# Two pairs of up-projection chunks per FFN in seven products for eight, and another beginning of the first FFN

## The chip, the cores and the metric

The kernel runs on one core of one Trainium2 chip. The metric is device time in microseconds of one execution; the lower, the better. The kernel before takes 1345.03 us (median of three runs, 1344.71 to 1345.4).

## What is computed

Two layers of a decoder trunk, for 256 tokens of width 1024, all in fp32. The change touches the two feed-forward networks (FFNs) of each layer, four in all:

```python
def swiglu(x, w1, w3, w2):
    return (jax.nn.silu(x @ w1) * (x @ w3)) @ w2
...
    for i in range(DEPTH):
...
        h = h + 0.5 * swiglu(rms_norm(h, g_ffn1[i]), w1_a[i], w3_a[i], w2_a[i])
        u = rms_norm(h, g_mix[i])
        h = h + hybrid_mixer(u, w_in[i], g_cq[i], g_ckv[i], w_uq[i], w_ukv[i],
...
        h = h + 0.5 * swiglu(rms_norm(h, g_ffn2[i]), w1_b[i], w3_b[i], w2_b[i])
        ple_gate = jax.nn.sigmoid(rms_norm(h, g_ple[i]) @ w_ple_gate[i])
        h = h + ple_gate * (p[i] @ w_ple_proj[i])
    return rms_norm(h, g_final)
```

DEPTH is 2, w1 and w3 are 1024 x 2816 and w2 is 2816 x 1024. `rms_norm` scales each token by one over its root mean square, and by a gain per channel.

## The kernel before

**Split numbers.** Every fp32 product is made of three matmuls on parts: a number is rounded to a high part, and the low part is the rest. `load` (L74 to 87) brings a weight tile of 128x1024 by a DMA that SyncE issues into `raw` (4 buffers). ScalarE casts it to `whi` (L85), VectorE subtracts to get `wlo` (L86); each has 7 buffers. `mm3` (L94 to 97) issues whi·xhi, wlo·xhi and whi·xlo, each a matmul of 128x512 for one K tile of 128. `split_T` (L126 to 129) does the same for tiles that are no weights.

**An FFN** (`ffn`, from L179). The 2816 columns are 11 chunks of 256. `up(c)` multiplies the tokens (two blocks of 128, `tb`) by the 256 columns of w1 and the 256 of w3 of a chunk: two PSUM banks of 128x512 from a pool of two (`mm`), each of 8 K tiles and 24 matmuls. The token's norm factor `r` is not in x: it is applied afterwards, in silu on ScalarE (L203, `act`) and in the gating on VectorE (L205, `pr`). `turn(c)` transposes the gated tile by four TensorE transposes into a bank of another pool of two (`tr`, L216) and splits it to `fhi` and `flo` (L128, L129). `down` multiplies by two tiles of w2 and adds up into four `acc` banks, which live for the whole FFN: 24 matmuls of 128x512 per chunk. So each chunk has 72 such matmuls and a turn.

**The order.** The loop goes through the chunks: up(c), turn(c-1), down(c-2). After the last chunk come turn(10), and down of chunks 9 and 10 together, bank by bank, chunk 9 ahead in each (L248 to 261); behind each bank the residual is added to h. The framework's scheduler puts the instructions of each engine in a fixed order, in which each engine then works them off, waiting on semaphores; TensorE, ScalarE, VectorE, GpSimd (POOL) and SyncE's DMA queue each have such a list of their own.

**The beginning** (`start`, L783 to 804). The first FFN's x comes transposed from a copy in memory (`xT`, four DMAs of 128x512), each followed by half of the first chunk's weights in pieces of 128x512. ScalarE and VectorE split x, scaled by the gain (L133, L134). The squares (`xsq`) are added up on POOL, and `start_r` (L807 to 816) sums them over the partitions by small matmuls with ones (L813), to get r. `soon` (L818) brings the identity matrix and h after chunk 1, `later` (L824) the constants of the mixer after chunk 3.

**Other places touched.** `ple_in` (L714) loads the embedding of the layer; `_layout` (L842) arranges the inputs on the host.

Of the kernel before, what the change touches and what calls it, by code (L numbers as in the profile page):

```python
# [8 lines left out]
F32 = mybir.dt.float32  # L9
# [5 lines left out]
P = 128  # L15
L = 2
# [17 lines left out]
def trunk(ctx: ExitStack, tc: tile.TileContext, a: dict, out: bass.AP):  # L34
# [26 lines left out]
    gcol = const("gcol", [P, L, 4, KT])  # L61
# [12 lines left out]
    def load(src, n=U, pool=None, step=U):  # L74
# [11 lines left out]
            V.tensor_tensor(out=lo[:, c], in0=raw[:, c], in1=hi[:, c].bitcast(F32), op=ALU.subtract)  # L86
        return hi, lo


    def behind(ins, table):  # L90
# [3 lines left out]
    def mm3(o, lhs, rhs, first, last):  # L94
        PE.matmul(o, lhs[0], rhs[0], start=first, stop=False)  # L95
        PE.matmul(o, lhs[0], rhs[1], start=False, stop=False)  # L96
        PE.matmul(o, lhs[1], rhs[0], start=False, stop=last)  # L97

    def bank(tag, bufs):
        return ps.tile([P, 512], F32, tag=tag, name=nm(tag), bufs=bufs)  # L100
# [1 line left out]
    def bank_mm():  # L102
        return bank("mm", 2)
# [4 lines left out]
    def bank_acc():  # L108
        return bank("acc", 4)
# [66 lines left out]
            pend.pop()()  # L176


    def ffn(li, w13, w2, r, g, first=False, aside=None):  # L179
        with tc.tile_pool(name=nm("fp"), bufs=3) as fp:  # L180
            if first:
                sq, un0 = start(fp)
            acc = []
            ffT = {}

            def up(c):
                nonlocal r
                un = un0 if first and c == 0 else [load(w13[li, c, i]) for i in range(4)]
                fhi = fp.tile([P, 2, S], F32R, tag="fhi", name=nm("fhi"), bufs=4)
                flo = fp.tile([P, 2, S], F32R, tag="flo", name=nm("flo"), bufs=4)  # L190
                ffT[c] = (fhi, flo)
                prs = []
                for tb in range(TB):
                    o = bank_mm()
# [5 lines left out]
                    if r is None:  # L200
                        r = start_r(sq)
                    act = fp.tile([P, FC], F32, tag="act", name=nm("act"))
                    A.activation(act, o[:, :FC], AF.Silu, scale=r[tb])  # L203
                    pr = fp.tile([P, FC], F32, tag="pr", name=nm("pr"), bufs=4)
                    V.scalar_tensor_tensor(  # L205
                        out=pr, in0=o[:, FC:], scalar=r[tb], in1=act, op0=ALU.mult, op1=ALU.mult
                    )
                    prs.append(pr)
                return prs

            def turn(c, prs):
                fhi, flo = ffT[c]
                t = bank_tr()
                for tb in range(TB):
                    for j in range(2):
                        PE.transpose(t[:, j * S + tb * P : j * S + (tb + 1) * P], prs[tb][:, j * P : (j + 1) * P], ident)  # L216
                split_T(t.rearrange("p (j t) -> p j t", j=2), fhi, flo)

            def load2(cs):
                return {c: [load(w2[li, 2 * c + j]) for j in range(2)] for c in cs}  # L220

            def down(cs, un, tb, n):
                for c in cs:
                    for j in range(2):
                        kt = 2 * c + j
                        f = [x[:, j, tb * P : (tb + 1) * P] for x in ffT[c]]
                        w = [x[:, n * 512 : (n + 1) * 512] for x in un[c][j]]
                        mm3(acc[2 * tb + n], f, w, kt == 0, kt == 2 * NFC - 1)

            prs = {}  # L230
            for c in range(NFC):
                prs[c] = up(c)
                if first and c == 1:
                    soon()
                if first and c == 3:
                    later()
                if c == 5 and aside is not None:
                    aside()
                if c == 1:
                    acc.extend(bank_acc() for _ in range(4))  # L240
                if c >= 1:
                    turn(c - 1, prs[c - 1])
                if c >= 2:
                    un = load2([c - 2])
                    for tb in range(TB):
                        for n in range(2):
                            down([c - 2], un, tb, n)
            turn(NFC - 1, prs[NFC - 1])  # L248
            cs = [NFC - 2, NFC - 1]
            un = load2(cs)  # L250
            ro = []
            for tb in range(TB):
                for n in range(2):
                    down(cs, un, tb, n)
# [458 lines left out]

    def ple_in(li, pool):  # L714
        pT = [pool.tile([P, 2, S], F32R, tag=f"pT{i}", name=nm("pT")) for i in range(2)]
        praw = pool.tile([P, 2, S], F32, tag="praw", name=nm("praw"))
        nc.sync.dma_start(praw, a["pT"][li])
        split_T(praw, *pT)
        return pT
# [60 lines left out]
                )  # L780
                nc.sync.dma_start(out[tb * P : (tb + 1) * P, 512:D], o[:, 512:D])

    def start(pool):  # L783
# [4 lines left out]
        un, sq = [], []  # L788
        for k in range(0, KT, 2):
            t = pool.tile([P, 2, S], F32, tag="xraw", name=nm("xraw"), bufs=4)  # L790
            nc.sync.dma_start(t, a["xT"][:, k : k + 2, :])
            q = pool.tile([P, 2, S], F32, tag="xsq", name=nm("xsq"), bufs=4)
            for j in range(2):
                split_g(
                    t[:, j, :].rearrange("p (b t) -> p b t", b=TB), xhi[:, :, k + j, :], xlo[:, :, k + j, :],
                    gcol[:, 0, 0, k + j : k + j + 1],
                )
            un.append(load(a["w13a"][0, 0, k // 2], step=512))
            if k < KT - 2:
                A.activation(q, t, AF.Square)  # L800
            else:
                V.tensor_tensor(out=q, in0=t, in1=t, op=ALU.mult)
            sq.append(q)
        return sq, un


    def start_r(sq):  # L807
        for t in sq[1:]:
            G.tensor_tensor(out=sq[0], in0=sq[0], in1=t, op=ALU.add)
        o = bank_acc()  # L810
        for tb in range(TB):
            for j in range(2):
                PE.matmul(o[:, tb : tb + 1], sq[0][:, j, tb * P : (tb + 1) * P], ones[:, 0:1], start=j == 0, stop=j == 1)  # L813
        ss = small("ss0", 2)
        V.tensor_copy(ss, o[:, 0:2])
        return [rsqrt_mean(ss[:, tb : tb + 1], D) for tb in range(TB)]

    def soon():  # L818
        nonlocal ident
        ident = const("ident", [P, P])  # L820
        for tb in range(TB):
            tc.keep_in_program_order(nc.sync.dma_start(h[tb], a["x"][tb * P : (tb + 1) * P, :]))
# [19 lines left out]
def _layout(i):  # L842
# [4 lines left out]
    c = np.ascontiguousarray  # L847
    o = {}
    o["x"] = c(f["x"].reshape(S, D))
    o["xT"] = c(f["x"].reshape(S, KT, P).transpose(2, 1, 0))  # L850
    o["pT"] = c(f["p"].reshape(L, S, 2, P).transpose(0, 3, 2, 1))

    def tiles(w, kk, ncol):
# [5 lines left out]
    for s in "ab":  # L859
        w1 = f[f"w1_{s}"].reshape(L, D, NFC, FC)  # L860
        w3 = f[f"w3_{s}"].reshape(L, D, NFC, FC)
        o[f"w13{s}"] = tiles(np.concatenate([w1, w3], 3).reshape(L, D, 2 * FF), 2, 512)
        o[f"w2{s}"] = c(f[f"w2_{s}"].reshape(L, 2 * NFC, P, D))
    win = f["w_in"]
    o["wz"] = c(win[:, :, :672].reshape(L, KT, P, 672))
    dq, dk, dv = (win[:, :, 672 + 512 * j : 672 + 512 * (j + 1)] for j in range(3))
# [55 lines left out]
```

## Time and profile before

| | |
|---|---|
| median of three runs | 1345.03 us |
| the profiled execution: its time | 1345.25 us |
| the profiled execution: its span | 1343.2 us |
| mean granted TensorE clock | 0.999 |
| moved by DMA | 236.61 MB, mean 176 GB/s |
| first three turns of the first FFN, in the chain of waits | at 33.13, 44.50 and 61.31 us |

The span goes from the first to the last instruction; 2.05 us of the time lie around it. In the rows of the trace, the first number is the start (in a timeline) and the second the length; `out<-in` names the tiles, `x` the count, and what stands in brackets is how long the engine had been idle, and what ended that. A matmul's recorded length is longer than its share of the pipelined engine: the distance between starts is what it costs.

```profile
PE   8999999999999999999999999999999999999997
DVE  6655565666768655555765555666766676555555
ACT  5544456665775644444654444566667836444445
DMA  7855547534455565555455555474444465655542
```

Each digit is the busy share of a fortieth of the span, in tenths.

### The profile page before, as it was taken

Reading aid. Unit: us, or ns where it says so; the run is one execution under the profiler, and the core shown is the slowest. Engines: PE = TensorE matmul, PEld = TensorE weight load, DVE = VectorE, ACT = ScalarE, POOL = GpSimd, SP = SyncE. Lnnn points to the kernel's source line nnn. Section 1 sums busy time; section 2 is a strip of 40 time slices with the busy share of each in tenths; the row PEclk is TensorE's granted clock in tenths of the full one; section 3 lists DMA queues with packets and bytes.
Section 4 is the critical chain, followed back from the end, with each engine's and each line's share of the span. In section 5 each row is a group of like instructions: output and inputs, shape, how many; then the busy total and the mean of one; then the engine's idle time right before and its main releaser. Section 6 shows DMA issues by size and latency. Waiting matters only on the chain.

```text
span 1343.2 us, 17893 instructions
## 1 busy us (share of the span) xinstructions
PE 1331.4 (99%) x6720; PEld 1114.3 (83%) x6720; DVE 816.0 (61%) x1190; ACT 735.2 (55%) x1122; POOL 50.3 (4%) x110
## 2 busy tenths in 40 slices
PE   8999999999999999999999999999999999999997
PEld 6888889978888888888888888898888788888886
DVE  6655565666768655555765555666766676555555
ACT  5544456665775644444654444566667836444445
POOL 2000000001100000000100000000010000000000
PEclk9999999999999999999999999999999999999999
DMA  7855547534455565555455555474444465655542
GB/s 269 275 187 188 187 131 222 176 112 144 138 170 173 167 207 188 188 187 189 159 188 188 188 188 188 133 224 138 157 141 143 142 208 160 199 189 191 184 158 82
DMA packets 68342, 236.61 MB, mean 176 GB/s; under 512 B 8224, under 2 KB 8864, under 8 KB 68256
## 3 DMA queue, kind: packets, MB, share of 16 engines
q1 hardware_dynamic: 67824, 234.43, 53.7%
q8 instruction: 52, 0.85, 0.3%
q10 hardware_dynamic: 432, 1.05, 0.2%
q14 instruction: 34, 0.28, 0.1%
HBM read 234.40 MB, written 1.05 MB: 175 GB/s over the span
## 4 chain that ended last, share of the span: by engine, by line
PE 95%; DVE 1%; ACT 1%; DMA 1%; issue 0%; SPq 0%; POOL 0%; POOLq 0%; ACTq 0%
PE mm L95 21%; PE mm L97 21%; PE mm L96 21%; PE acc L95 8%; PE acc L97 8%; PE acc L96 8%; PE tr L216 1%; PE tr L143 1%; PE tr L512 1%; DVE wlo L86 1%; ACT whi L85 1%; PE acc L614 1%; PE acc L596 1%; PE acc L486 1%; DMA xraw<-in_xT 1%; PE tr L475 0%
## 5 line engine op out<-in xcount | busy, mean ns | idle before, releaser
L86 DVE TENSOR_TENSOR wlo<-raw,whi 128x1024 fp32r<-128x1024 f32 (+3 forms) x450 | 534.0, 1200 | 252.8 <-ACT whi L85 235.5
L85 ACT CAST whi<-raw 128x1024 fp32r<-128x1024 f32 (+3 forms) x450 | 456.5, 1029 | 260.2 <-PE acc L97 134.9
L95 PE MATMUL mm<-whi,xhi 128*128 128x512 f32 (+1 forms) x1032 | 403.7, 392 | 1.7 <-ACT whi L85 1.2
L96 PE MATMUL mm<-wlo,xhi 128*128 128x512 f32 (+1 forms) x1032 | 401.7, 390 | 0.7 <-DVE wlo L86 0.7
L97 PE MATMUL mm<-whi,xlo 128*128 128x512 f32 (+1 forms) x1032 | 401.7, 389 | 0.0
L95 PEld LDWEIGHTS mm<-whi,xhi 128*128 128x128 f32 x1032 | 193.8, 188 | 43.1 <-ACT whi L85 1.9
L96 PEld LDWEIGHTS mm<-wlo,xhi 128*128 128x128 f32 x1032 | 194.0, 188 | 41.1 <-DVE wlo L86 2.5
L97 PEld LDWEIGHTS mm<-whi,xlo 128*128 128x128 f32 x1032 | 193.8, 188 | 40.2 <-DVE xlo L129 0.9
L95 PE MATMUL acc<-whi,fhi 128*128 128x512 f32 x352 | 140.9, 402 | 0.0
L203 ACT ACTIVATE act<-mm,r 128x256 f32<-128x256 f32 x88 | 41.8, 475 | 176.7 <-PE mm L97 172.5
L97 PE MATMUL acc<-whi,flo 128*128 128x512 f32 x352 | 137.2, 392 | 0.0
L96 PE MATMUL acc<-wlo,fhi 128*128 128x512 f32 x352 | 136.8, 390 | 0.0
L205 DVE SCALAR_TENSOR_TENSOR pr<-mm,r,act 128x256 f32<-128x256 f32 x88 | 42.3, 481 | 130.7 <-ACT act L203 130.7
L97 PEld LDWEIGHTS acc<-whi,flo 128*128 128x128 f32 x352 | 66.0, 188 | 14.7
L95 PEld LDWEIGHTS acc<-whi,fhi 128*128 128x128 f32 x352 | 66.2, 188 | 13.2 <-ACT fhi L128 1.0
L96 PEld LDWEIGHTS acc<-wlo,fhi 128*128 128x128 f32 x352 | 66.3, 188 | 12.7
L95 PE MATMUL mm<-xhi,whi 128*128 128x256 f32 x256 | 73.9, 289 | 0.0
L97 PE MATMUL mm<-xhi,wlo 128*128 128x256 f32 x256 | 72.4, 283 | 0.0
L96 PE MATMUL mm<-xlo,whi 128*128 128x256 f32 x256 | 72.4, 283 | 0.0
L95 PEld LDWEIGHTS mm<-xhi,whi 128*128 128x128 f32 x256 | 48.9, 191 | 2.0 <-ACT eT L514 0.7
L96 PEld LDWEIGHTS mm<-xlo,whi 128*128 128x128 f32 x256 | 49.0, 191 | 0.0
L97 PEld LDWEIGHTS mm<-xhi,wlo 128*128 128x128 f32 x256 | 48.9, 191 | 0.0
(211 smaller groups left out, 1350.9 us busy)
## 6 DMA issues: line engine op xcount, KB each, us to landing
raw<-in_w13b SPq DMA_DIRECT2D x88, 512.0 KB, 4.5
raw<-in_w13a SPq DMA_DIRECT2D x84, 512.0 KB, 4.5
raw<-in_wg SPq DMA_DIRECT2D x48, 512.0 KB, 4.1
raw<-in_w2a SPq DMA_DIRECT2D x44, 512.0 KB, 4.3
raw<-in_w2b SPq DMA_DIRECT2D x44, 512.0 KB, 4.3
raw<-in_wqk SPq DMA_DIRECT2D x32, 512.0 KB, 4.3
raw<-in_wo SPq DMA_DIRECT2D x24, 512.0 KB, 4.3
raw<-in_wv SPq DMA_DIRECT2D x16, 512.0 KB, 4.4
```

The lines of the kernel that those rows point to most:

```text
L85: A.copy(hi[:, c], raw[:, c])
L86: V.tensor_tensor(out=lo[:, c], in0=raw[:, c], in1=hi[:, c].bitcast(F32), op=ALU.subtract)
L95: PE.matmul(o, lhs[0], rhs[0], start=first, stop=False)
L96: PE.matmul(o, lhs[0], rhs[1], start=False, stop=False)
L97: PE.matmul(o, lhs[1], rhs[0], start=False, stop=last)
L143: PE.transpose(t[:, j * P : (j + 1) * P], h[tb][:, k * P : (k + 1) * P], ident)
L203: A.activation(act, o[:, :FC], AF.Silu, scale=r[tb])
L205: V.scalar_tensor_tensor(out=pr, in0=o[:, FC:], scalar=r[tb], in1=act, op0=ALU.mult, op1=ALU.mult)
L216: PE.transpose(t[:, j * S + tb * P : j * S + (tb + 1) * P], prs[tb][:, j * P : (j + 1) * P], ident)
L486: PE.matmul(o[:, P : 3 * P], q[:, P : 2 * P], k, start=True, stop=True)
L512: PE.transpose(t[:, j * P : (j + 1) * P], e[:, j * P : (j + 1) * P], ident)
L596: PE.matmul(os[i][:, c], k, q, start=True, stop=True)
```

## The change

**Pairs of chunks.** Chunks 7 and 8, and chunks 9 and 10, go through one matrix product of 2x2 blocks: the blocks of x are (token block) x (half of the 1024 channels), those of the weights (half of the channels) x (chunk). Seven products of such blocks are made in place of eight, each with 4 K tiles, so 12 matmuls of 128x512 (`products`). That needs sums and differences of blocks. For x they are made once per FFN (`x_forms`), after token block 1 is scaled by the ratio of the two blocks' norm factors, which a matmul of ones with a diagonal matrix spreads over the partitions; so one r serves both token blocks. For the weights, four differences of two tiles each are made per pair on VectorE (`form`), and each of the seven operands is split (`make`). The results are put together by additions of 128x512 that read the PSUM bank (`add`), and one copy on ScalarE.

**Order.** Chunks 0 to 2 go as before. Then come two blocks of eight steps (`block`): in each, seven products alternate with single weight tiles (`up_unit`) of two plain chunks (3 and 4; 5 and 6), and with down units of one w2 tile. At the end stand down(5), turns 6 and 10, down(6), turn 9, and down of chunks 9 and 10, bank by bank.

**Beginning.** x and the weights of chunk 0 come together in eight DMAs of 128x768 (`xw`). r comes from h by `norm_r` as in the other stages; h's two DMAs stand between weight tiles of chunk 1. Chunk 0 keeps its two banks until r is there, and chunk 1 goes into two `acc` banks. The gain comes by ScalarE's DMA queue. `start_r`, the squares and `soon` are gone. The embedding's tile is taken from a pool of scratch tiles.

Core of the diff:

```diff
+            def up_unit(c, i, os):
+                un = load(w13[li, c, i])
+                if i == 0:
+                    os.extend(bank_mm() for _ in range(TB))
+                for tb in range(TB):
+                    for kt in (2 * i, 2 * i + 1):
+                        w = [x[:, (kt % 2) * 512 : (kt % 2) * 512 + 512] for x in un]
+                        mm3(os[tb], x_at(tb, kt), w, kt == 0, kt == KT - 1)
+                if i == 3:
+                    for tb in range(TB):
+                        gated(c, tb, os[tb], r[tb])
...
+            def down_unit(c, j):
+                w = load(w2[li, 2 * c + j])
+                for tb in range(TB):
+                    for n in range(2):
+                        down(c, j, w, tb, n)
...
+            def x_forms():
+                rho = small("rho")
+                V.reciprocal(rho, r[0])
+                V.tensor_tensor(out=rho, in0=rho, in1=r[1], op=ALU.mult)
+                dg = scratch()[:, :P]
+                V.tensor_scalar_mul(dg, ident, rho)
+                o = bank_tr()
+                PE.matmul(o[:, :P], ones, dg, start=True, stop=True)
+                rb = fp.tile([P, P], F32, tag="rb", name=nm("rb"), bufs=1)
+                A.copy(rb, o[:, :P])
...
+                for t, tb, n in ((a10, 1, 0), (a11, 1, 1), (a00, 0, 0), (a01, 0, 1)):
+                    c = slice(4 * n, 4 * n + 4)
+                    V.tensor_tensor(
+                        out=v4(t), in0=xhi[:, tb, c, :].bitcast(F32), in1=xlo[:, tb, c, :].bitcast(F32), op=ALU.add
+                    )
+                    if tb:
+                        V.tensor_tensor(out=v4(t), in0=v4(t), in1=rb[:, None, :].to_broadcast([P, 4, P]), op=ALU.mult)
...
+                V.tensor_tensor(out=s1, in0=a10, in1=a11, op=ALU.add)
+                f[5] = quarter(s1)
+                sub(s1, s1, a00)
+                f[6] = quarter(s1)
+                sub(a10, a00, a10)
+                f[7] = quarter(a10)
+                sub(a01, a01, s1)
+                f[3] = quarter(a01)
+                f[4] = quarter(a11)
...
+                def form(i):
+                    for u, w in enumerate(ws):
+                        if i == 1:
+                            sub(w[0, 0], w[0, 1], w[0, 0])
+                        elif i == 2:
+                            t2s.append(wtile())
+                            sub(t2s[u], w[1, 1], w[0, 0])
+                        elif i == 3:
+                            sub(w[0, 1], w[1, 1], w[0, 1])
+                        else:
+                            sub(w[1, 0], w[1, 0], t2s[u])
...
+                def products():
+                    o = bank_tr()
+                    product(o, 1, True)
+                    m1 = t512("m1")
+                    A.copy(m1, o)
+                    yield
+                    product(o, 2)
+                    gated(c, 0, o, r[0])
+                    yield
+                    o = bank_tr()
+                    product(o, 6, True)
+                    u2 = t512("u2")
+                    add(u2, o, m1)
+                    yield
+                    product(o, 7)
+                    add(m1, o, m1)
+                    yield
...
+                for k in range(8):
+                    if k < 6:
+                        make((2, 6, 7, 5, 3, 4)[k])
+                    if k < 3:
+                        form(k + 2)
...
+                    if k < 7:
+                        next(ps)
...
+                    up_unit(plain[k // 4], k % 4, os)
+                    if k in downs:
+                        down_unit(*downs[k])
+                    for t in turns.get(k, ()):
+                        turn(t)
...
+            for j in range(2):
+                down_unit(5, j)
+            turn(6)
+            turn(10)
+            for j in range(2):
+                down_unit(6, j)
+            turn(9)
+            un = {(c, j): load(w2[li, 2 * c + j]) for c in (9, 10) for j in range(2)}
```

**ScalarE at the end of the first FFN.** Before: `tr_298` is the turn of chunk 9, `tr_305` that of chunk 10, the `whi` are casts of weights.

```order
L203 ACTIVATE act_296_1457<-mm_295_1432,r_31_207 128x256
L85 CAST whi_340_1638<-raw_339_1637 128x1024
L128 CAST fhi_263_1274<-tr_298_1461 128x512
L85 CAST whi_343_1644<-raw_342_1643 128x1024
L85 CAST whi_346_1650<-raw_345_1649 128x1024
L128 CAST fhi_290_1401<-tr_305_1504 128x512
```

Now: `tr_346` is the turn of chunk 6, `tr_349` of chunk 10, `tr_358` of chunk 9.

```order
L86 CAST whi_393_1734<-raw_392_1733 128x1024
L135 CAST fhi_344_1544<-tr_346_1546 128x512
L135 CAST fhi_347_1553<-tr_349_1555 128x512
L86 CAST whi_396_1740<-raw_395_1739 128x1024
L86 CAST whi_399_1746<-raw_398_1745 128x1024
L135 CAST fhi_356_1598<-tr_358_1600 128x512
```

A weight cast stands right ahead of the last turned tile's cast in both. What moved is on TensorE, at the same place. Before, behind the last turn (`tr_305`, its tile is `fhi_290`):

```order
L216 MATMUL tr_305_1504<-ident_326,pr_297_1459 128x128 x2
L95 MATMUL acc_57_330<-whi_307_1512,fhi_263_1274 128x512
L96 MATMUL acc_57_330<-wlo_308_1513,fhi_263_1274 128x512
L97 MATMUL acc_57_330<-whi_307_1512,flo_264_1275 128x512
L95 MATMUL acc_57_330<-whi_310_1518,fhi_263_1274 128x512
L96 MATMUL acc_57_330<-wlo_311_1519,fhi_263_1274 128x512
L97 MATMUL acc_57_330<-whi_310_1518,flo_264_1275 128x512
L95 MATMUL acc_58_331<-whi_307_1512,fhi_263_1274 128x512
L95 MATMUL acc_57_330<-whi_313_1524,fhi_290_1401 128x512
```

Now, around the last turn (`tr_358`, its tile is `fhi_356`):

```order
L102 MATMUL acc_58_321<-whi_354_1581,fhi_344_1544 128x512
L103 MATMUL acc_58_321<-wlo_355_1582,fhi_344_1544 128x512
L104 MATMUL acc_58_321<-whi_354_1581,flo_345_1545 128x512
L250 MATMUL tr_358_1600<-ident_228,pr_252_1111 128x128 x2
L250 MATMUL tr_358_1600<-ident_228,pr_324_1444 128x128 x2
L102 MATMUL acc_55_318<-whi_360_1608,fhi_356_1598 128x512
```

Before, seven matmuls that read an older tile stand between the last turn and the first use of its tile; now none does.

**VectorE at the start of the first block,** second FFN: `pr_1104` is the gated tile of chunk 2, the `wr` are weight tiles of the pair and their forms, the `wlo` splits.

```order
L136 TENSOR_TENSOR wlo_1109_4782<-wr_1076_4665,whi_1108_4781 128x1024
L136 TENSOR_TENSOR wlo_1111_4786<-wr_1080_4669,whi_1110_4785 128x1024
L87 TENSOR_TENSOR wlo_1114_4793<-raw_1112_4791,whi_1113_4792 128x1024
L238 SCALAR_TENSOR_TENSOR pr_1104_4770<-mm_1102_4743,r_1012_4427,act_1103_4768 128x256
L136 TENSOR_TENSOR flo_1106_4773<-tr_1107_4774,fhi_1105_4772 128x512
L320 TENSOR_TENSOR wr_1076_4665<-wr_1077_4666,wr_1076_4665 128x1024
L320 TENSOR_TENSOR wr_1080_4669<-wr_1081_4670,wr_1080_4669 128x1024
L87 TENSOR_TENSOR wlo_1117_4811<-raw_1115_4809,whi_1116_4810 128x1024
L136 TENSOR_TENSOR wlo_1119_4828<-wr_1078_4667,whi_1118_4827 128x1024
L136 TENSOR_TENSOR wlo_1121_4832<-wr_1082_4671,whi_1120_4831 128x1024
```

Where before weight splits and gated tiles alternated, four splits of the pair and two forms now stand among them.

**VectorE in the beginning,** now: `xlo` and the first `wlo` belong to chunk 0, `wlo_23` to `wlo_32` to chunk 1, `pr_46` and `pr_48` are the gated tiles of chunk 0.

```order
L136 TENSOR_TENSOR wlo_16_139<-wr_18_146,whi_15_138 128x512
L293 TENSOR_TENSOR wr_63_331<-xhi_68,xlo_69 128x512
L87 TENSOR_TENSOR wlo_23_204<-raw_21_202,whi_22_203 128x1024
L293 TENSOR_TENSOR wr_64_332<-xhi_68,xlo_69 128x512
L87 TENSOR_TENSOR wlo_26_211<-raw_24_209,whi_25_210 128x1024
L238 SCALAR_TENSOR_TENSOR pr_46_254<-mm_19_152,r_38_239,act_45_252 128x256
L269 RECIPROCAL rho_59_322<-r_38_239 128x1
L270 TENSOR_TENSOR rho_59_322<-rho_59_322,r_44_250 128x1
L87 TENSOR_TENSOR wlo_29_218<-raw_27_216,whi_28_217 128x1024
L238 SCALAR_TENSOR_TENSOR pr_48_258<-mm_20_177,r_44_250,act_47_256 128x256
```

Two weights of chunk 1 (`wlo_29` and the one behind `pr_48`) now stand behind operations that read r; before, r was read behind one of chunk 1's.

More of the change, by code (lines that the diff above doesn't have):

```diff
@@ L87, in load, with split_w @@
         return hi, lo
+    def split_w(w):
+        hi = wp.tile([P, U], F32R, tag="whi", name=nm("whi"), bufs=7)
+        lo = wp.tile([P, U], F32R, tag="wlo", name=nm("wlo"), bufs=7)
+        split_T(w, hi, lo)
+        return hi, lo
     def behind(ins, table):
@@ L92, in behind, with mm3 @@
         tc.add_manual_dep(ins.ins, table.ins.name, order, reason="behind")
[L94 to L97, printed above, removed]
+    def mm3(o, lhs, rhs, first, last, **more):
+        PE.matmul(o, lhs[0], rhs[0], start=first, stop=False, **more)
+        PE.matmul(o, lhs[0], rhs[1], start=False, stop=False, **more)
+        PE.matmul(o, lhs[1], rhs[0], start=False, stop=last, **more)
     def bank(tag, bufs):
@@ L179, in ffn, with wtile, t512, up @@
     def ffn(li, w13, w2, r, g, first=False, aside=None):
+        nonlocal ident
         with tc.tile_pool(name=nm("fp"), bufs=3) as fp:
+            def wtile():
+                return fp.tile([P, U], F32, tag="wr", name=nm("wr"), bufs=10)
+            def t512(name):
+                return fp.tile([P, 512], F32, tag="t512", name=nm(name), bufs=4)
             if first:
-                sq, un0 = start(fp)
+                un0 = start(wtile)
             acc = []
             ffT = {}
[L186 to L192, printed above, removed]
+            prs = {}
+            def up(c, un, bank):
+                os = []
                 for tb in range(TB):
-                    o = bank_mm()
+                    o = bank()
                     for kt in range(KT):
@@ L199, in up, with gated, turn @@
                             settle()
[L200 to L212, printed above, removed]
+                    os.append(o)
+                    if r is not None:
+                        gated(c, tb, o, r[tb])
+                return os
+            def up_unit(c, i, os):
[9 more added lines that the diff above has]
+                        gated(c, tb, os[tb], r[tb])
+            def gated(c, tb, o, scale):
+                act = fp.tile([P, FC], F32, tag="act", name=nm("act"), bufs=2)
+                A.activation(act, o[:, :FC], AF.Silu, scale=scale)
+                pr = fp.tile([P, FC], F32, tag="pr", name=nm("pr"), bufs=6)
+                V.scalar_tensor_tensor(
+                    out=pr, in0=o[:, FC:], scalar=scale, in1=act, op0=ALU.mult, op1=ALU.mult
+                )
+                prs[c, tb] = pr
+            def turn(c):
+                fhi = fp.tile([P, 2, S], F32R, tag="fhi", name=nm("fhi"), bufs=4)
+                flo = fp.tile([P, 2, S], F32R, tag="flo", name=nm("flo"), bufs=4)
+                ffT[c] = (fhi, flo)
                 t = bank_tr()
@@ L222, in down @@
[L222 to L232, printed above, removed]
-                if first and c == 1:
[L234 to L238, printed above, removed]
+            def down(c, j, w, tb, n):
+                kt = 2 * c + j
+                f = [x[:, j, tb * P : (tb + 1) * P] for x in ffT[c]]
+                mm3(acc[2 * tb + n], f, [x[:, n * 512 : (n + 1) * 512] for x in w], kt == 0, kt == 2 * NFC - 1)
@@ new lines, in ffn @@
+            for c in range(3):
+                if first and c == 1:
+                    un = []
+                    for i in range(4):
+                        un.append(load(w13[li, c, i]))
+                        if i < 2:
+                            load_h(i)
+                    ident = const("ident", [P, P])
+                    r = [norm_r(tb) for tb in range(TB)]
+                    for tb, o in enumerate(os0):
+                        gated(0, tb, o, r[tb])
+                    up(c, un, bank_acc)
+                else:
+                    os0 = up(c, un0 if first and c == 0 else [load(w13[li, c, i]) for i in range(4)], bank_mm)
@@ L239, in ffn @@
                 if c == 1:
                     acc.extend(bank_acc() for _ in range(4))
+                    fx = x_forms()
+                    wg = winograd(7, fx)
                 if c >= 1:
[L242 to L249, printed above, removed]
@@ L250, in ffn @@
-            un = load2(cs)
+                    turn(c - 1)
+            wg[0](1)
+            wg[1](1)
+            for j in range(2):
+                down_unit(0, j)
+            if first:
+                later()
+            wg = block(
+                wg, (3, 4), {0: [2], 4: [3]},
+                {0: (1, 0), 1: (1, 1), 2: (2, 0), 3: (2, 1), 5: (3, 0), 6: (3, 1)}, 9,
+            )
+            if aside is not None:
+                aside()
+            block(
+                wg, (5, 6), {0: [4], 1: [7], 2: [8], 5: [5]},
+                {1: (4, 0), 2: (4, 1), 3: (7, 0), 4: (7, 1), 5: (8, 0), 6: (8, 1)},
+            )
@@ L793, in start @@
             for j in range(2):
[L794 to L804, printed above, removed]
@@ L807, in start_r @@
[L807 to L822, printed above, removed]
+                t = wtile()[:, : S + 512]
@@ new lines, in start @@
+                nc.sync.dma_start(t, a["xw"][:, k + j, :])
+                src = t[:, :S].rearrange("p (b t) -> p b t", b=TB)
+                xh, xl = xhi[:, :, k + j, :], xlo[:, :, k + j, :]
+                g = gcol[:, 0, 0, k + j : k + j + 1]
+                if k == 0:
+                    V.tensor_scalar_mul(xh, src, g)
+                    V.scalar_tensor_tensor(
+                        out=xl, in0=src, scalar=g, in1=xh.bitcast(F32), op0=ALU.mult, op1=ALU.subtract,
+                    )
+                else:
+                    split_g(src, xh, xl, g)
```

95 lines of the change are left out of this document (82 added, 13 removed).

## The prediction

> **What bounds the kernel now.** I read the page first: busy time, then the shares of the chain that ended last.
>
> ```profile
> span 1343.2 us, 17893 instructions
> PE 1331.4 (99%) x6720; PEld 1114.3 (83%) x6720; DVE 816.0 (61%) x1190; ACT 735.2 (55%) x1122; POOL 50.3 (4%) x110
> PE 95%; DVE 1%; ACT 1%; DMA 1%; issue 0%; SPq 0%; POOL 0%; POOLq 0%; ACTq 0%
> L86 DVE TENSOR_TENSOR wlo<-raw,whi 128x1024 fp32r<-128x1024 f32 (+3 forms) x450 | 534.0, 1200 | 252.8 <-ACT whi L85 235.5
> ```
>
> TensorE is busy for 99% of the span and is 95% of the chain. VectorE has 39% free and waits mostly for ScalarE's casts. So removed matmuls count in full, as long as VectorE and ScalarE, which get more work, still deliver weights in time. Next, the price of a matmul, from the timeline of TensorE inside one up chunk, and a window over a whole FFN:
>
> ```profile
> 67.07 0.39 PE L95 MATMUL mm<-whi,xhi 128*128 128x512 f32 x1
> ...
> 77.72 0.39 PE L97 MATMUL mm<-whi,xlo 128*128 128x512 f32 x1
> 77.95 0.60 PE L216 MATMUL tr<-ident,pr 128*128 128x128 f32 x4
> 78.31 0.48 PE L95 MATMUL acc<-whi,fhi 128*128 128x512 f32 x1
> ```
> ```profile
> 470.00:640.00 170.00, 170.00 (x771) 140.41 (x771) 88.70 (x94) 75.94 (x94) 0.64 (x3) 1.00 0.58 190
> ```
>
> From 67.07 to 77.72 lie 47 starts, so one 128x512 matmul costs 10.65 / 47 = 0.2266 us, whatever its recorded 0.39. A turn of four transposes costs 78.31 - 77.95 = 0.36. In the window (columns: busy time and count of PE, PEld, DVE, ACT, POOL, then clock, DMA share, GB/s) TensorE never stops, at granted clock 1.00. VectorE is busy 88.7 of 170, and the DMA engines 0.58: there is room for both.
>
> All sums below are made against the profiled execution, 1345.25 us (span 1343.2 and 2.05 around it); the median of the runs is 1345.03, so the two are interchangeable here.
>
> **1. Matmuls removed: -21.75.** A pair of chunks has 2 x 48 = 96 products of the form 128x512; by seven products for eight it has 84. Two pairs in each of four FFNs: 8 x 12 = 96 matmuls fewer, 96 x 0.2266 = 21.75 us.
>
> **2. Work added on TensorE: +0.9.** Each FFN gets one matmul with ones that spreads the ratio of the two norms over the partitions. The nearest row is a chain step of the same shape:
>
> ```profile
> 209.16 0.45 PE tr L279 x4
> ```
>
> Two such matmuls stand in that step; I take 0.22 each, 0.9 for four; bounds 0.4 to 1.8.
>
> **3. Beginning of the first FFN: -4.6.** What it takes now:
>
> ```profile
> 21.70 0.50 PE mm L95
> 33.13 0.44 PE tr L216 x4
> ```
> ```profile
> 16.63 1.05 PE L813 MATMUL acc<-ones,xsq 128*128 128x1 f32 x8 [0.18 <-POOL xsq L809]
> 21.70 0.50 PE L95 MATMUL mm<-whi,xhi 128*128 128x512 f32 x1 [0.48 <-DVE pr L205]
> ```
> ```profile
> 5.40 0.88 DVE L134 SCALAR_TENSOR_TENSOR xlo<-xraw,gcol,xhi 128x256 fp32r<-128x256 f32 x2 [5.40 <-ACT xhi L133]
> 6.37 0.69 DVE L86 TENSOR_TENSOR wlo<-raw,whi 128x512 fp32r<-128x512 f32 x1
> ...
> 13.65 1.78 DVE L86 TENSOR_TENSOR wlo<-raw,whi 128x512 fp32r<-128x512 f32 x1
> 15.35 1.91 DVE L134 SCALAR_TENSOR_TENSOR xlo<-xraw,gcol,xhi 128x256 fp32r<-128x256 f32 x2
> ```
>
> The first turn comes at 33.13, after 96 matmuls worth 21.75. Before, TensorE pays for the norm (16.63: small matmuls; 21.70: no free bank until a gated tile is made), and VectorE's last operations before that took 1.78 and 1.91 for shapes that take 0.69 and 0.88 elsewhere, while POOL added squares. After, POOL's additions of squares and the small matmuls are gone, and chunk 1 goes into other banks. What is late next is VectorE: it begins at 5.4 with 2 scalings and 8 differences of 128x256 (0.44 each, half of the 0.88), 8 subtractions of 128x512 (0.6) and, in the same queue, two of the four additions of the forms (0.6): 4.4 + 4.8 + 1.2 = 10.4, so the last piece is ready at 15.8. The last group of six matmuls then ends at about 17.2, and 48 x 0.2266 = 10.9 us later chunk 1 ends, at 28.1. I add 0.4: behind the gated tile of chunk 0, which waits for the norm, stand two weight subtractions of chunk 1 (see the order), and the norm now waits for h, which arrives between weight tiles. So 28.5 for 33.13: -4.6. Bounds: -5.5 (28.1, and the x-forms' additions hidden) and 0 (the norm 4 us later, at about 25).
>
> **4. End of each FFN: +9.2 in all.** Before, the last turn is covered:
>
> ```profile
> 183.81 0.39 PE L97 MATMUL acc<-whi,flo 128*128 128x512 f32 x1
> ...
> 184.72 0.60 PE L216 MATMUL tr<-ident,pr 128*128 128x128 f32 x4
> 185.07 0.48 PE L95 MATMUL acc<-whi,fhi 128*128 128x512 f32 x1
> ...
> 186.54 0.72 PE L95 MATMUL acc<-whi,fhi 128*128 128x512 f32 x2
> ```
> ```profile
> 184.23 2.00 ACT L85 CAST whi<-raw 128x1024 fp32r<-128x1024 f32 x2 [3.34 <-PE acc L97]
> 186.13 0.58 ACT L128 CAST fhi<-tr 128x512 fp32r<-128x512 f32 x1
> ```
>
> ScalarE starts two weight casts at 184.23, when a matmul frees their buffers, and only then the cast of the turned tile (186.13); TensorE meanwhile does matmuls of the chunk before, until 186.54. After the change, the down units of chunk 6 stand right behind turns 6 and 10, those of chunk 9 right behind turn 9, and need just these turned tiles; nothing else can run. In ScalarE's queue one weight cast, which waits for the last matmul of the preceding down unit, stands ahead of each (the order shows both). For turn 9: the matmul frees the buffer 0.19 after the turn begins (0.39 recorded, less the pitch of 0.2266, and 0.03 from 183.81 + 0.39 to 184.23); cast 0.95 (half of 1.90, from 184.23 to 186.13); turned tile 0.58; so TensorE resumes at 1.74, not 0.36: **1.35 lost** (rounded down, since matmuls read the tile's first half first). For turns 6 and 10 the same 1.74 against 2 x 0.36 = 0.72: 1.0. Sum 2.35 x 4 = 9.4, less some 0.2 of such waiting in before. Bounds: 0 if ScalarE takes its instructions in another order, (2.35 + 2 x 0.95) x 4 = 17 if two casts came ahead each time, as at 184.23.
>
> **5. VectorE at the beginning of the pairs: +4.0.** Per pair of chunks VectorE gets 14 splits instead of 8, and 8 forms, all of 128x1024; per FFN it also gets 25 operations of 128x512 or near it, for the x-forms and for adding up the products. Prices:
>
> ```profile
> 453.23 1.23 DVE L86 TENSOR_TENSOR wlo<-raw,whi 128x1024 fp32r<-128x1024 f32 x1 [1.79 <-ACT whi L85]
> 454.38 1.28 DVE L147 TENSOR_TENSOR xg<-tr,gcol 128x512 f32<-128x512 f32 x2
> 455.57 1.21 DVE L86 TENSOR_TENSOR wlo<-raw,whi 128x1024 fp32r<-128x1024 f32 x1
> 456.71 1.28 DVE L129 TENSOR_TENSOR xlo<-xg,xhi 128x512 fp32r<-128x512 f32 x2
> ```
> ```profile
> L86 DVE TENSOR_TENSOR wlo<-raw,whi 128x1024 fp32r<-128x1024 f32 x420 | 507.4, 1223 | 236.4 <-ACT whi L85 221.4
> L85 ACT CAST whi<-raw 128x1024 fp32r<-128x1024 f32 x420 | 435.1, 1051 | 253.7 <-PE acc L97 133.4 <-PE mm L97 86.8 <-PE mm L96 23.3
> L203 ACT ACTIVATE act<-mm,r 128x256 f32<-128x256 f32 x88 | 41.8, 475 | 176.7 <-PE mm L97 172.5 <-POOL r L124 4.1
> L205 DVE SCALAR_TENSOR_TENSOR pr<-mm,r,act 128x256 f32<-128x256 f32 x88 | 42.3, 481 | 130.7 <-ACT act L203 130.7
> ```
>
> Back to back, a wide operation takes 1.14 (455.57 to 456.71), and one of 512 takes half of 1.20 (454.38 to 455.57 for two); I use 0.62, and 0.45 for 256. Over the whole FFN this fits. Eleven chunks last 11 x (72 x 0.2266 + 0.36) = 183 us, of which VectorE is busy 52% (88.7 of 170), some 95 us; (112 x 1.14 + 99 x 0.62) / 4 = 47 us come on top. The tight place is the start of block 1. From behind the gated tile that ends chunk 1 to the weights of chunk 3's third unit, VectorE's order has 23 wide operations, 14 of 512 and 3 of 256: 23 x 1.14 + 14 x 0.62 + 3 x 0.45 = 36.3 us. TensorE's order has 156 matmuls, three turns and the ones step there: 156 x 0.2266 + 3 x 0.36 + 0.22 = 36.7 us; but VectorE starts 1.1 later, by the matmul's end (0.17 beyond its pitch), 0.475 on ScalarE and the gated tile's own 0.48. So it is 36.3 + 1.1 - 36.7 = 0.7 late in FFNs 2, 3 and 4. In the first a 24th wide operation, a weight of chunk 2, stands in the stretch: 1.9. That makes 3 x 0.7 + 1.9 = 4.0. Bounds: 0, since some of the waiting matmuls can be others', and 26 (the slower side below). Behind this place VectorE has less per unit and gets ahead again. ScalarE has 45% free, and 48 more casts of 1.05 are 12.6 us per FFN; the bytes of the weights do not change.
>
> **Sum:** 1345.25 - 21.75 + 0.9 - 4.6 + 9.2 + 4.0 = **1333.0 us**.
>
> **Rivals.**
>
> *Covers hold (B).* Terms 4 and 5 are nothing: 1345.25 - 21.75 + 0.9 - 4.6 = 1319.8. For it: VectorE at 61%, and the existing FFN end loses next to nothing. Against it: the order leaves TensorE no matmul behind turn 9.
>
> *Full durations (C).* If each wide operation held VectorE for its recorded 1.22 rather than 1.14, the tight place is 23 x 0.08 = 1.85 later in each FFN, 7.4 in all: 1340.4. The rows speak against it, with starts 1.14 apart. For it speaks that the x-forms and forms here often read what the operation just ahead has written, which no quoted pair does. The Trainium skill has this rule in "VectorE: DVE Perf Modes", section "The DRAIN you can't avoid": the next operation does not start until the pipe has emptied, and only one that is not held starts earlier. By the rule the whole kernel would come out at C; the quoted rows, 1.14 apart behind an operation of 1.21, agree with its exception only.
>
> *The start gains nothing (E).* The norm late, as bounded in 3: 1333.0 + 4.6 = 1337.6.
>
> *The slower side (D): each subtraction waits for its own cast.* In before, runs of VectorE's splits are often paced by ScalarE:
>
> ```profile
> 470.62 1.22 DVE L86 TENSOR_TENSOR wlo<-raw,whi 128x1024 fp32r<-128x1024 f32 x1 [0.16 <-ACT whi L85]
> 488.37 3.95 DVE L86 TENSOR_TENSOR wlo<-raw,whi 128x1024 fp32r<-128x1024 f32 x3 [1.45 <-ACT whi L85]
> ```
>
> A form, its cast and its subtraction are one chain across two engines. With 1.22 + 0.16 = 1.38 per wide operation instead of 1.14, the tight place is 23 x 0.24 = 5.5 longer per FFN, 22 in all: 1355.0. It decides from 1.27 on (1345.25 - 1333.0 = 12.25, and 12.25 / 4 / 23 = 0.133 above 1.14); the triple at 488.37 has 3.95 / 3 = 1.32. Against it: forms and x-forms between the splits need no cast and give ScalarE time to get ahead.
>
> *That products aren't saved* can't be: the order counts 4584 matmuls of 128x512 for 4680.
>
> **Chances.** Forecast 0.62 (1327 to 1339 by its own terms), B 0.14, E 0.07, C 0.09, D 0.08. A measurement of this kernel can tell about 0.2%, 2.7 us, from no change, so faster means below 1342.3. Everything but D and the upper edge of C does that: faster 0.88, same 0.05, slower 0.07. The range runs from B to just above C, 1319 to 1341, and leaves out D and half of B.
>
> **What would show it.** Term 1: 96 fewer 128x512 matmuls at an unchanged pitch. Term 3: the first turn near 28.5. Term 4: in each FFN, just ahead of the last two groups of down units, TensorE idle for 1.0 and 1.35 with a cast of the turned tile as releaser. Term 5: waits for a subtraction in the first 37 us after chunk 1, under 1 us per FFN (1.9 in the first), and VectorE at about 1020 us busy. The prediction is wrong if TensorE shows gaps in the middle of the blocks, if the products wait for a bank (the copy or addition that empties it), or if the ends show none.

## The result and the profile after

| | before | after |
|---|---|---|
| median | 1345.06 us (4 runs, 1344.71 to 1345.4) | 1333.43 us (4 runs, 1332.72 to 1334.1) |
| profiled execution | 1345.25 us | 1332.86 us |
| its span | 1343.2 us | 1331.1 us |

The ratio is 0.9913, with a 95% interval of 0.9898 to 0.9928: 0.9% faster. The forecast was 1333.0 us.

The page of the changed kernel, first the span and the busy times, then the shares of the chain that ended last:

```profile
span 1331.1 us, 17969 instructions
PE 1312.2 (99%) x6624; PEld 1097.5 (82%) x6624; DVE 994.0 (75%) x1414; ACT 802.8 (60%) x1205; POOL 50.2 (4%) x109
PE 94%; ACT 2%; DVE 2%; DMA 1%; issue 1%; POOL 0%; SPq 0%; POOLq 0%; ACTq 0%; DVEq 0%
```

TensorE is still the bound: it has 96 instructions less and is 19.2 us less busy. VectorE has 178 us more to do (about 204 were counted) and hides nearly all of it. The view of TensorE's waits lists what is not hidden (total us, times, longest):

```profile
PE acc L102 <- ACT fhi L135: 7.7, 8, 1.2
PE tr L992 <- POOL mhalf L72: 1.0, 1, 1.0
PE acc L103 <- DVE wlo L87: 0.9, 2, 0.5
PE tr L102 <- ACT m L352: 0.6, 1, 0.6
```

Eight waits for a turned tile, two in each FFN, stand out. In before, the same list comes to 4.0 us in all, and no matmul in it waits for `fhi`. The chain of the changed kernel, at the beginning of the first FFN and at its end (start, length):

```profile
18.98 0.57 POOL r L175
...
21.93 0.56 POOL r L175
22.60 1.24 DVE wlo L87
23.88 0.50 PE acc L103
29.41 0.44 PE tr L250 x4
```
```profile
171.78 0.90 ACT whi L86
172.74 0.59 ACT fhi L135
173.37 0.50 PE acc L102
...
179.16 1.04 ACT whi L86
180.20 0.49 ACT fhi L135
180.74 0.50 PE acc L102
```

The first turn begins at 29.41 for 33.13. At the end, each time a weight cast, then the turned tile's cast, and then TensorE: the order that the section on the change shows.

### The profile page after: what moved, and what is told of

Same layout as the page of the kernel before. It is cut to its first block, busy times and chain, and to the rows that moved or that the text cites. A ratio compares the mean times of both kernels' runs of the same rounds, so it can differ in the third digit from the quotient of the medians.

```text
span 1331.1 us, 17969 instructions
## 1 busy us (share of the span) xinstructions
PE 1312.2 (99%) x6624; PEld 1097.5 (82%) x6624; DVE 994.0 (75%) x1414; ACT 802.8 (60%) x1205; POOL 50.2 (4%) x109
## 4 chain that ended last, share of the span: by engine, by line
PE 94%; ACT 2%; DVE 2%; DMA 1%; issue 1%; POOL 0%; SPq 0%; POOLq 0%; ACTq 0%; DVEq 0%
PE mm L102 17%; PE mm L104 17%; PE mm L103 17%; PE acc L102 8%; PE acc L103 8%; PE acc L104 8%; PE tr L104 4%; PE tr L102 4%; PE tr L103 4%; PE tr L250 1%; PE tr L150 1%; ACT whi L86 1%; PE tr L716 1%; DVE wlo L87 1%; DMA h<-in_x 1%
## 5 line engine op out<-in xcount | busy, mean ns | idle before, releaser
L87 DVE TENSOR_TENSOR wlo<-raw,whi 128x1024 fp32r<-128x1024 f32 (+1 forms) x378 | 450.1, 1201 | 137.3 <-ACT whi L86 135.1
L86 ACT CAST whi<-raw 128x1024 fp32r<-128x1024 f32 (+1 forms) x378 | 387.3, 1035 | 198.2 <-PE mm L104 77.5
L102 PE MATMUL mm<-whi,xhi 128*128 128x512 f32 (+1 forms) x760 | 296.0, 393 | 0.0
L103 PE MATMUL mm<-wlo,xhi 128*128 128x512 f32 (+1 forms) x760 | 295.1, 389 | 0.3 <-DVE wlo L87 0.3
L104 PE MATMUL mm<-whi,xlo 128*128 128x512 f32 (+1 forms) x760 | 295.2, 389 | 0.0
L103 PEld LDWEIGHTS mm<-wlo,xhi 128*128 128x128 f32 x760 | 142.9, 188 | 28.9 <-DVE wlo L87 0.8
L135 ACT CAST whi<-wr 128x1024 fp32r<-128x1024 f32 (+1 forms) x120 | 121.6, 1023 | 66.9 <-PE acc L104 38.9
L136 DVE TENSOR_TENSOR wlo<-wr,whi 128x1024 fp32r<-128x1024 f32 (+1 forms) x120 | 140.6, 1185 | 24.8 <-ACT whi L135 23.6
L320 DVE TENSOR_TENSOR wr<-wr,wr 128x1024 f32<-128x1024 f32 x64 | 76.3, 1217 | 0.0
L102 PE MATMUL tr<-whi,q 128*128 128x512 f32 x160 | 63.7, 398 | 0.0
L104 PE MATMUL tr<-whi,q 128*128 128x512 f32 x160 | 62.6, 391 | 0.0
```

The costliest lines, as they stand in the source:

```text
L86: A.copy(hi[:, c], raw[:, c])
L102: PE.matmul(o, lhs[0], rhs[0], start=first, stop=False, **more)
L103: PE.matmul(o, lhs[0], rhs[1], start=False, stop=False, **more)
L104: PE.matmul(o, lhs[1], rhs[0], start=False, stop=last, **more)
L135: A.copy(hi, t)
L136: V.tensor_tensor(out=lo, in0=t, in1=hi.bitcast(F32), op=ALU.subtract)
```

## Experiments

**The saved matmuls put back.** The first product of each pair is issued twice.

```diff
                     product(o, 1, True)
+                    product(o, 1, True)
```

> The first of the seven products is issued twice in each pair (its second start overwrites the first): 8 x 12 = 96 more matmuls of 128x512, the number that the change saves. If TensorE is the bound inside the blocks, each costs 0.2266 us: +21.75 on 1333.4, less what they cover of the waits at the start of block 1 (some 3 us in the trace): 1352 to 1355. Rival: the blocks are bound by VectorE, and a matmul more is hidden there: under +10, below 1343.

Measured: 1352.59 us (1352.34 to 1353.11), +19.2 on the changed kernel. By the marks of the chain (the first transposes behind each FFN) the second, third and fourth FFN are 5.44, 5.45 and 5.41 us longer: 24 x 0.2266 = 5.44, the full price, so the blocks are bound by TensorE. The first FFN is only 3.4 longer. There the added matmuls cover 1.6 of the waits at the start of block 1 (TensorE loses 1.25 from 28 to 75 us, 2.88 in the changed kernel), and the first turn begins 0.4 earlier (29.02 for 29.41).

**The turns at the end moved ahead.**

```diff
-            for j in range(2):
-                down_unit(5, j)
-            turn(6)
-            turn(10)
+            down_unit(5, 0)
+            turn(6)
+            turn(9)
+            down_unit(5, 1)
             for j in range(2):
                 down_unit(6, j)
-            turn(9)
```

Turn 10 goes into the block's list of turns, behind its last unit.

> The last three turns are moved ahead: turn 10 behind the last unit of the block, turns 6 and 9 between the two down units of chunk 5, so that at least 12 matmuls (2.7 us) stand between each turn and the first use of its tile. If the two waits per FFN (1.06 + 1.42 and 0.1 behind each, 2.7) come from ScalarE's weight cast ahead of the turned tile's, they go: -9.5 to -10.8, 1322.6 to 1323.9. Rival: ScalarE's two casts of turned tiles, now ahead, make the weight casts behind them late, and the wait comes back on a weight: less than 3 gained, above 1330.

Measured: 1323.12 us (1322.34 to 1323.19), ratio to the kernel before 0.9837 (0.9823 to 0.9852): 10.3 less than the changed kernel. By the marks behind the FFNs each gives 2.6 to 2.8; 0.8 is lost again in the second layer's mixer, at the same `kf`. The timeline of ScalarE in this run, at the end of the first FFN:

```profile
169.66 1.05 ACT L86 CAST whi<-raw 128x1024 fp32r<-128x1024 f32 x1 [1.31 <-PE acc L104]
170.61 1.07 ACT L135 CAST fhi<-tr 128x512 fp32r<-128x512 f32 x2
173.26 1.05 ACT L86 CAST whi<-raw 128x1024 fp32r<-128x1024 f32 x1 [1.59 <-PE acc L104]
```

A weight cast still stands ahead of the two turned tiles, but they are done at 171.7, and TensorE, which has the second down unit of chunk 5 to do, does not wait at all. The rival falls: no wait came back on the weights. This version beats both kernels.

**VectorE loaded early in the block.**

```diff
                             sub(t2s[u], w[1, 1], w[0, 0])
+                            if c == 7:
+                                sub(t2s[u], w[1, 1], w[0, 0])
```

> The two subtractions of the second form (128x1024) are done twice in the first block: two more wide operations on VectorE per FFN, in the stretch that I called tight. If VectorE has no slack there, each costs its 1.14: 2 x 1.14 x 4 = 9.1, less a few tenths of slack per FFN: +7 to +9, 1340.5 to 1342.5. Rival: the waits there come from one order of semaphores and not from the amount of work: under +1.5.

Measured: 1336.27 us (1335.73 to 1336.75), +2.8: neither 7 nor nothing. By the marks of the chain the four FFNs are 0.4, 0.5, 0.6 and 0.5 longer, and the rest, 1.0, is lost in the second layer's mixer, whose code is the same (a wait of 0.8 for `kf` that the changed kernel does not have). So 2.27 us of work cost 0.5, and some 1.7 us of room were found, of which the expectation had none. In the second FFN TensorE's order shows where: behind the turn in this stretch, twelve matmuls of product 2 stand ahead of the first one that needs a new low part, and four in the changed kernel. Eight more are 1.8 us.

**The same load late in the block.**

```diff
                     fw[i] = [split_w(t2s[u] if i == 6 else w[at[i]]) for u, w in enumerate(ws)]
+                    if c == 7 and i == 4:
+                        for u, w in enumerate(ws):
+                            hi, lo = fw[i][u]
+                            V.tensor_tensor(out=lo, in0=w[1, 0], in1=hi.bitcast(F32), op=ALU.subtract)
```

> The same two wide operations on VectorE per FFN, but at the sixth step of the first block (the low parts of the last operand of the pair are subtracted twice). By my account VectorE is ahead there by 5 us or more: 0, 1333.0 to 1334.0. Rival: VectorE's sum of work is the bound over the whole block: +9, as in the run with the early place.

Measured: 1333.12 us (1332.81 to 1333.32): 0. VectorE's work is free there.

**Twice as much early.** The loop does the second form three times instead of twice.

```diff
-                            sub(t2s[u], w[1, 1], w[0, 0])
+                            for _ in range(3 if c == 7 else 1):
+                                sub(t2s[u], w[1, 1], w[0, 0])
```

> As the run with two more wide operations early in the first block, but four of them per FFN. Two cost 2.84 in all, far less than 9.1; so some 1.6 us of slack per FFN must have been there, and the next two find none: 2 x 1.14 = 2.27 per FFN, +6.8 (three FFNs) to +9.1 (four) on 1336.27: 1343 to 1345.4. Rival: each costs a part, because the scheduler orders other matmuls ahead as it did for two: another +2.8, about 1339.

Measured: 1347.05 us (1345.47 to 1348.09), +10.8 on the run with two, above the range. TensorE's waits in this run, and its timeline in the first FFN:

```profile
PE mm L103 <- DVE wlo L87: 9.5, 4, 2.7
```
```profile
58.36 0.79 PE L103 MATMUL mm<-wlo,xhi 128*128 128x512 f32 x1 [2.67 <-DVE wlo L87]
58.95 0.63 PE L104 MATMUL mm<-whi,xlo 128*128 128x512 f32 x1
59.38 0.63 PE L102 MATMUL mm<-whi,xhi 128*128 128x512 f32 x1
59.80 0.63 PE L103 MATMUL mm<-wlo,xhi 128*128 128x512 f32 x1
```

One wait per FFN, 9.5 us in all. By the marks the second and the fourth FFN are 2.3 longer than with two operations, just the 2 x 1.14 expected; the first and the third are 3.3 and 3.6 longer. What comes on top there is the clock. Behind the wait, matmuls start 0.43 apart and not 0.2266, in the first and the third FFN, though not in the second and fourth. The windows show it (columns as before; the clock is the last but two):

```profile
56.00:58.00 2.00, 0.00 (x0) 0.00 (x0) 2.00 (x3) 1.79 (x2) 0.00 (x0) 1.00 0.00 0
58.00:59.00 1.00, 0.64 (x2) 0.55 (x3) 1.00 (x2) 1.00 (x2) 0.00 (x0) 0.51 0.00 0
59.00:60.00 1.00, 1.00 (x4) 0.81 (x3) 1.00 (x3) 1.00 (x2) 0.00 (x0) 0.50 0.70 94
...
62.00:63.00 1.00, 1.00 (x6) 0.82 (x5) 1.00 (x2) 0.00 (x0) 0.00 (x0) 1.00 0.74 299
```

**The beginning alone.** The kernel before, with the new beginning of the first FFN:

```diff
-                prs[c] = up(c)
-                if first and c == 1:
-                    soon()
+                if first and c == 1:
...
+                    r = [norm_r(tb) for tb in range(TB)]
+                    prs[0] = [gated(o, r[tb]) for tb, o in enumerate(prs[0])]
+                    prs[c] = up(c, un, bank_acc)
```

> The kernel before with only the new beginning of the first FFN (x and weights in one stream, r from h, chunk 0 held in its banks, chunk 1 in two acc banks). The first turn of the changed kernel begins at 29.4, of which 0.2 is the ones step, for 33.1 before: -3.7 to -4.0, since nothing behind it is changed: 1341.0 to 1341.3. Rival: what is gained there is lost again in the next chunks, whose weights come no sooner: -1 or less, above 1344.

Measured: 1340.12 us (1339.83 to 1340.93) beside 1344.91 for the kernel before, ratio 0.9965 (0.9952 to 0.9978): -4.8, more than expected. The first turn comes in two halves in this run, two transposes at 22.54 and two at 27.78; the matmul behind it starts at 27.92 (33.33 in the same view of before, 5.4 later), and the marks behind all four FFNs stay 5.2 to 5.4 ahead. So the beginning by itself gives some 5, and about 1.3 is lost again in the changed kernel, between 21.77 and 24.21, as waits and slow starts that this run does not have. The norm is late there. POOL's first operation of it (128x1) takes 3.05 us in the changed kernel and 0.30 in this run, so that the norm of block 0 is there at 19.54 for 17.20. First the changed kernel, then this run:

```profile
15.48 3.05 POOL L171 TENSOR_SCALAR ss<-ss 128x1 f32<-128x1 f32 x1 [14.53 <-ACT junk L164]
17.26 1.22 DVE L87 TENSOR_TENSOR wlo<-raw,whi 128x1024 fp32r<-128x1024 f32 x1
```
```profile
14.47 1.23 DVE L87 TENSOR_TENSOR wlo<-raw,whi 128x1024 fp32r<-128x1024 f32 x1 [0.58 <-ACT whi L86]
15.45 0.30 POOL L165 TENSOR_SCALAR ss<-ss 128x1 f32<-128x1 f32 x1 [14.49 <-ACT junk L158]
```

POOL's operation ends 0.05 behind VectorE's in both, at 18.53 behind 18.48 and at 15.75 behind 15.70. In the changed kernel VectorE works without a gap up to 18.48, with the x-forms' additions between the splits; here it stops at 15.70. So the x-forms do take the 1.3, but by way of POOL; that VectorE holds POOL up is read from these times and was not tested by itself. Behind the late norm, VectorE multiplies the norms' ratio only at 22.52, and a weight of chunk 1 stands right behind it:

```profile
22.52 0.16 DVE L270 TENSOR_TENSOR rho<-rho,r 128x1 f32<-128x1 f32 x1 [1.89 <-POOL r L175]
22.60 1.22 DVE L87 TENSOR_TENSOR wlo<-raw,whi 128x1024 fp32r<-128x1024 f32 x1
```

**The forms left out.**

```diff
-                        if i == 1:
-                            sub(w[0, 0], w[0, 1], w[0, 0])
-                        elif i == 2:
-                            t2s.append(wtile())
-                            sub(t2s[u], w[1, 1], w[0, 0])
...
+                        if i == 2:
+                            t2s.append(w[1, 1])
```

> The changed kernel without the 64 subtractions of weight tiles that make the forms (the operands of the products are the plain tiles, so what is computed is not the reference's), all splits, products and the x-forms stay. VectorE is freed of 16 x 1.14 = 18 us per FFN. If its work costs only where TensorE waits for a subtraction at the start of block 1, it gives back 0.3 in each of three FFNs and at most 1.7 in the first, whose wait for the copy stays: -0.5 to -2.6, 1330.8 to 1332.9. Rival: the added work on VectorE slows the blocks elsewhere too: -5 or more, below 1328.5.

Measured: 1336.07 us (1335.25 to 1336.76): slower than with the forms, which neither theory had. So something else must have changed with it. ScalarE's timeline in the first FFN, and TensorE's:

```profile
53.03 0.47 ACT L236 ACTIVATE act<-tr,r 128x256 f32<-128x256 f32 x1 [1.98 <-PE tr L104]
53.40 1.98 ACT L86 CAST whi<-raw 128x1024 fp32r<-128x1024 f32 x2
```
```profile
54.49 0.73 PE L102 MATMUL mm<-whi,xhi 128*128 128x512 f32 x2 [1.50 <-ACT whi L86]
55.75 0.50 PE L103 MATMUL mm<-wlo,xhi 128*128 128x512 f32 x1 [0.53 <-DVE wlo L87]
```

The scheduler, with the forms gone, put the activation behind product 2 ahead of two weight casts. ScalarE waited for product 2 for 1.98 us, TensorE then for the weights, and the granted clock was 0.50 from 56.2 to 59.6 us. To see whether that is all, the activation was held behind the casts of the next operand:

```diff
-                    gated(c, 0, o, r[0])
+                    gated(c, 0, o, r[0], casts[-1] if first and c == 7 else None)
...
+                if after is not None:
+                    behind(silu, after)
```

> As the run without the form subtractions (the result is again not the reference's), but in the first FFN ScalarE's activation behind product 2 is held behind the casts of the next operand, where the changed kernel has it. In the run without forms the scheduler had put it ahead of two casts of plain weights; TensorE then waited 1.5 and 0.5 us for them at 54 us, and its clock stood at half for 3 us. If that one place explains the loss, it goes (2.1 us by the marks at the end of that FFN), and the gain of the missing forms shows: 1331 to 1334. Rival: leaving the forms out costs by itself, by an earlier use of buffers or of the DMA: 1335.5 to 1336.5 again.

Measured: 1332.51 us (1331.66 to 1332.72). The loss in the first FFN was that one place. Without the forms, 18 us of VectorE's work per FFN, the first FFN ends 1.7 earlier than in the changed kernel, and the other three gain nothing more; in the second layer's mixer 1.3 of it is lost again, 0.9 of that as a wait for `kf`. The medians are 0.9 apart, the two profiled executions 0.1 (1332.72 and 1332.86). TensorE's loss in the first FFN's stretch from 29 to 65 us falls from 2.85 to 0.94: the forms are what it waits for there. The `kf` wait comes and goes between kernels with the same mixer; its cause stays open.

## Why the prediction was right, point by point

"Saved" and "lost" are sums of starts in TensorE's timeline against the pitch of 0.2266.

| term | forecast | measured | from |
|---|---|---|---|
| 1 matmuls removed | -21.75 | -21.75 | 5.44 per FFN, put back |
| 2 ones step | +0.9 | +0.9 | 0.22 each |
| 3 beginning | -4.6 | -3.9 | 33.13 to 29.41 less the ones step |
| 4 ends of FFNs | +9.2 | +10.3 | 2.7 per FFN, less 0.1 each in before |
| 5 VectorE at block 1 | +4.0 | +3.5 | 2.6 in the first FFN, 0.3 in each other |
| sum | -12.25 | -10.95 | |
| profiled executions | | -12.39 | |

The terms measured leave 1.4 us over. 0.3 is the time around the span (2.05 before, 1.76 after), some 0.4 lies between the FFNs by the marks of the chain, and the rest in differences of 0.1 per FFN that I did not trace. That the forecast of 1333.0 came within 0.4 of the median is therefore partly luck: terms 3 to 5 together were 1.3 too low, and these 1.4 made up for it.

**Term 1** was right, price and place. The pitch of the matmuls is the old one:

```profile
506.60 0.39 PE L102 MATMUL mm<-whi,xhi 128*128 128x512 f32 x1
...
512.49 0.39 PE L104 MATMUL tr<-whi,q 128*128 128x512 f32 x1
```

26 intervals in 5.89 us are 0.2265 each, products of the pair among them.

**Term 3** was 0.7 too large. The step that was mis-sized is the allowance of 0.4 for the norm, which cost 1.3: 0.76 as waits and the rest as slower starts around them, behind POOL's operation of 3.05 us, which the forecast did not have. Chunk 0 itself ended at 16.8 (17.2 worked out), and VectorE's last piece was ready at 15.0 (15.8 forecast). The run of the beginning alone shows the bound of -5.5 (x-forms hidden) to be about what it gives by itself.

**Term 4** was right in mechanism and place, and a little small. Behind turns 6 and 10 TensorE loses 1.06 and then 0.1, behind turn 9 1.42 and 0.1: 2.7 per FFN for 2.35. The chain gives the parts: casts begin 171.78 and 172.74, 0.96 apart, and TensorE starts 0.63 behind the second, for 0.95 and 0.58. The three parts of the forecast (0.19, 0.95 and 0.58) add up to 1.72, not 1.74. The rounding down was wrong, and the first matmul behind a wait costs 0.1 more. That the wait is made by TensorE's order, and not by ScalarE's amount of work, is shown by the run with the turns ahead.

**Term 5** was near in its sum by luck, with errors that cancel. VectorE's time was as counted: in the second FFN it works without a gap from 476.57, behind the gated tile, to 512.91, when the weight in question is ready. That is 36.34 us; 36.3 was forecast.

```profile
476.57 1.29 DVE L297 TENSOR_TENSOR wr<-wr,rb 128x512 f32<-128x512 f32 x2
...
511.69 1.22 DVE L87 TENSOR_TENSOR wlo<-raw,whi 128x1024 fp32r<-128x1024 f32 x1
```
```profile
477.00:515.00 38.00, 38.00 (x172) 31.13 (x172) 37.90 (x43) 24.22 (x30) 0.00 (x0) 1.00 0.66 232
```

VectorE is busy for 37.90 of 38.00 us there, and still TensorE does not stop. The step that failed is "So it is 36.3 + 1.1 - 36.7 = 0.7 late in FFNs 2, 3 and 4": it lets the unit need its low part with its first matmul. In TensorE's timeline three matmuls that need only the high part, or another tile, come first:

```profile
512.72 0.61 PE L102 MATMUL mm<-whi,xhi 128*128 128x512 f32 x2
513.17 0.39 PE L102 MATMUL acc<-whi,fhi 128*128 128x512 f32 x1
513.39 0.39 PE L103 MATMUL mm<-wlo,xhi 128*128 128x512 f32 x1
```

The low part, ready at 512.91, is used at 513.39: 0.5 early, not 0.7 late. Of these 1.2, 0.7 is the three matmuls, and the rest is that TensorE itself comes to this unit later than worked out, at 512.72 for 512.1. What is lost in these FFNs (0.3) lies earlier, at 488, at the first down unit. In the run with two more operations the scheduler ordered more of product 2's matmuls ahead of such low parts, which is how 2.3 us of work could cost 0.5; with four operations the order was the same and the room used up. In the first FFN the loss was larger, 2.6 for 1.9: a wait of 0.56 for the copy of product 1, which stands behind two weight casts on ScalarE, and three smaller ones for low parts. A product that waits for the copy is one of the signs by which the prediction said it would be wrong; it came once, in this FFN alone. Leaving the forms out took that wait and two of the three others away, so VectorE's added work is behind this loss.

**The rivals.** B (no stalls) is refuted by the eight waits; the run with the turns ahead comes near to its time, 1323.1 for 1319.8, since most of its gain is then made. C and D (a wide operation takes 1.22, or 1.38) are refuted by the 36.34 us. E (the beginning gains nothing) is refuted by the run of the beginning alone. The Trainium skill's rule in "VectorE: DVE Perf Modes", section "The DRAIN you can't avoid", would have each operation wait for an empty pipe; wide operations that start 1.14 apart here, with forms and splits in one queue, are of the kind that the page itself excepts as not held. Where an operation reads what the one ahead has written, the start came later by about a tenth (478.37 to 479.09 is 0.72, for 0.60), too few times to matter.

## What to carry to other kernels

Saved work on the bound engine counts in full only if the new order keeps cover behind each hand-over. Here 22 us were saved and 10 given back at four places, where a tile was used right behind the transposes that make it; moving three calls gave them back again. Look at the order of the engine that casts: a cast that waits for a buffer holds up all that stand behind it. And count when each part of an operand is first read: an engine can be busy for nearly all of a stretch, as VectorE is here for 37.90 of 38 us, and cost only 0.3. Work that fills the last gaps of one engine can still hold up another: the additions for the x-forms went with a norm that came 2.3 us later on POOL.

## What was not expected of the hardware

A wait of TensorE of 1.5 to 2.7 us was enough, in some cases, to halve its clock for some 3.4 us: granted clock 0.50 and starts 0.43 apart, after a wait of 2.67 us in the first FFN and one of 2.29 in the third, but not after 2.29 and 2.26 in the second and fourth, in one and the same execution. In the run without forms it followed waits of 1.50 and 0.53 close together. The waits of 0.74 and 1.18 at the ends of the FFNs never did it in these traces. "TensorE: Matmul & The Clock Gate" of the Trainium skill, section "What's actually happening", has the clock drop after an idle window of about 3.4 us, and says that the windows run freely. It fits this that of two equal waits one dropped the clock and the other did not. The figure does not agree: the longest of these waits was 2.67 us.

Small operations of POOL took longer when VectorE was at a wide subtraction. In the changed kernel the operations that scale and add up a norm's sums (128x1) take 0.19 to 0.27 us where VectorE is idle. The longest took 3.05, as shown above; another, at 324.46, took 1.22 and ended at 325.68, where VectorE's subtraction ended at 325.63.
